# Starting every tile that matmuls read at a multiple of 128 bytes

## The chip, the cores and the metric

The kernel runs on one core of a Trainium2 chip. The metric is the device time of one execution in microseconds, and of several executions the median.

## The reference

One decoder layer, batch 1, 1024 tokens of width 1024, all in float32:

```python
h = rmsnorm(x, norm_mix)
q, kc, vc, ks, vs, kw, vw, nsa_g, rq, rk, rv, rg, gate_a, gate_b = split(h @ w_in)     # 5400 columns
nsa = NSA(rotary(q), ...)            # 8 heads of 64, 2 key groups: compressed blocks, selected blocks, window of 512
ret = retention(rotary(rq), rotary(rk), rv)   # 4 heads of 128, chunks of 128 tokens
mix = sigmoid(gate_a) * (nsa @ w_proj_a) + sigmoid(gate_b) * ((silu(rg) * ret) @ w_proj_b)
x = x + mix @ w_out
x = x + square(relu(rmsnorm(x, norm_mlp) @ w_up)) @ w_down        # hidden width 4096
y = rmsnorm(x, norm_final)
```

The top 16 of 16 key blocks are selected, so the selected branch is plain causal attention over all keys.

## The kernel before

**How a product is made.** Each float32 factor is split into a high part of a shorter type (`float32r`) and the rest: `wh` and `wl` from a raw weight tile `raw`, `bh` and `bl` for the 1024 x 1024 activations, `QQ` and `ql` for queries, `ph` and `pl` for probabilities. A product is then three matmuls: high by high, high by low, low by high. Every matmul goes through one helper, `mm` on line 153, `mm(o, w, m, start, stop)`: `w` is the stationary operand (up to 128 x 128, loaded into the array, PEld in the profile), `m` the moving one (128 x up to 512, streamed through it). In the profile's names the moving operand stands first, where the two have different names: `mm<-wh,bh` streams `wh` past `bh`, and `gps<-bh,wh` streams `bh` past `wh`.

```python
def dense_tok(o, j, W, k0=0, k1=KD, ticks=True):
    js = slice(j * P, (j + 1) * P)
    for k in range(k0, k1):
        h, l = W[k]
        mm(o, bh[:, k, js], h, k == 0, False)
        mm(o, bh[:, k, js], l, False, False)
        mm(o, bl[:, k, js], h, False, k == KD - 1)
```

**Stages, in the order of time.**

- Up to about 372 us: `dense_tok` multiplies tiles of 128 tokens with 512 columns of `w_in` (24 matmuls of 128 x 512 a call), for retention (two chunks of heads, each with a first loop over 8 token tiles for q and k, and a second loop for v and g), then for the compressed and selected keys and values, the window keys (280 columns), and the queries. Retention's own small matmuls (`pS`, `pO`, `pD`), transposes (`tp`, `pZ`) and the compression's matmuls (`pc`, 128 x 256) stand between calls or in the middle of one.
- 372 to 777 us: attention. Scores `S` stream keys (`KKs`, `KKw`) past `QQ` and `ql`; probabilities `pS`, `pW` are transposed against `ident` into `pt`, split into `ph`, `pl`, and streamed past `Vs`, `Vw`, `Vc` into `O`. Threes of gate matmuls (`gps`) are put between them by a written-out order.
- 777 to 864 us: the two projections, from `Ah`, `Al`, `Bh`, `Bl`.
- 864 to 964 us: `w_out` by `dense_tok` again, into `mmu`, with the second norm and its transposes.
- 964 to 1265 us: `w_up`, by seven products in place of eight (`mmu`), which stream `bh`, `bl` and `t2h` to `t4l`.
- 1265 us to the end: `w_down`, again seven products (`mmd`).

PE's order is the order of the code. The other engines' instructions are ordered by the code or by a scheduler when the program is built.

**Where tiles lie.** Tile pools take space in each partition from the left end upwards, or from the right end downwards (`side="right"`), and a pool that is closed gives its space to the next. Tiles start at multiples of 32 bytes. The left side starts at a multiple of 128 with `ident` (512 bytes), `small` (64) and `nhalf` (16, which take 32), 608 bytes in all, which is 96 more than a multiple of 128; the right end is itself 96 over a multiple of 128. Weights are split into slots of several pools in turn; up to 372 us

```python
wrx = es.enter_context(tc.tile_pool(name="wrx", bufs=3, reuse_waits="tile"))
use_ring(wrx, wring, wrx, wring, wrx)
```

so that of five slots three are in `wrx`, which lies behind the table `cret` (2848 bytes, 32 over a multiple of 128), and two in `wring`, which lies ahead of it. Where the operands of matmuls start, counted from the last multiple of 128 bytes, in the built program before:

| tiles | start before | start after |
|---|---|---|
| `bh`, `bl`, `KKs`, `KKw`, `Vs`, `Vw`, `Vc`, `qt`, `qkT`, `t2h` to `t4l` (right side) | 96 | 0 |
| `wh`, `wl` in `wring`, `wr4`, `wr5`, `wr7`; `Ah` to `Bl`; `h2` | 96 | 0 |
| `wh`, `wl` in `wrx` and `wr2` | 0 | 0 |
| `QQ`, `ql`, `ph`, `pl`, `pS`, `pW` (behind `cmp_m`, 480 bytes) | 64 | 0 |
| `ident`; retention's `qk`, `s`, `v`, `n`, `sd`, `z`; `xh`, `xl`, `hh`, `kd`, `cd` | 0 | 0 |
| first norm's `h` | 0 | 32 |
| `warm`, `one`, `irow` | 0 | 64 |

For shortness a matmul is called 0/96 where its moving operand starts at 0 and its stationary one at 96. Of the 5,528 `float32r` matmuls with 512 columns 4,632 are 96/96 before, 720 are 0/96 (all up to 372 us, `wh` in `wrx` past `bh`) and 176 are 96/64 (`S`). Of those with 256 columns `O` is 64/96 (592), and `pc` is 0/0 (96). The matmuls of 280 columns read the second half of a slot, which starts 96 bytes further on.

Of the kernel before, what the change touches and what calls it, by code (L numbers as in the profile page):

```python
# [9 lines left out]
F32 = mybir.dt.float32  # L10
F32R = mybir.dt.float32r
I32 = mybir.dt.int32
AF = mybir.ActivationFunctionType
# [4 lines left out]
P = 128  # L18
# [93 lines left out]
def hybrid_block(ctx: ExitStack, tc: tile.TileContext, a: dict, out: bass.AP):  # L112
    nc = tc.nc
    V, A, G, T = nc.vector, nc.scalar, nc.gpsimd, nc.tensor
    ctx.enter_context(tc.manual_schedule(engines={mybir.EngineType.PE}))

    cst = ctx.enter_context(tc.tile_pool(name="cst", bufs=1, reuse_waits="tile"))
    dram = ctx.enter_context(tc.tile_pool(name="scr", bufs=1, space=DRAM))
    bigs = ctx.enter_context(ExitStack())
    big = bigs.enter_context(tc.tile_pool(name="big", bufs=1, side="right", reuse_waits="tile"))  # L120
    wraw = ctx.enter_context(tc.tile_pool(name="wraw", bufs=3, reuse_waits="tile"))
    wring = ctx.enter_context(tc.tile_pool(name="wring", bufs=2, reuse_waits="tile"))
# [9 lines left out]
    bl = big.tile([P, KD, S], F32R, name="bl")  # L132
    ident = cst.tile([P, P], F32, name="ident")
    small = cst.tile([P, 16], F32, name="small")
    nhalf = cst.tile([P, 4], F32, name="nhalf")
    V.memset(nhalf, -0.5)
    clock = {"t": 0, "n": 0}
    due = []
# [94 lines left out]
    with ExitStack() as es:  # L233
        psA = es.enter_context(tc.tile_pool(name="psA", bufs=2, space=PSUM, reuse_waits="tile"))
        tabs = es.enter_context(tc.tile_pool(name="tabs", bufs=1, reuse_waits="tile"))
        cret = tabs.tile([P, P + 512 + 72], F32, name="cret")
        cosr = tabs.tile([P, NT, 64], F32, name="cosr")
        sinr = tabs.tile([P, NT, 64], F32, name="sinr")
        cosn = tabs.tile([P, NT, 8], F32, name="cosn")
# [5 lines left out]
        with ExitStack() as e1:  # L245
# [4 lines left out]
            nrm = nrms.enter_context(tc.tile_pool(name="nrm", bufs=2, side="right", reuse_waits="tile"))  # L250
# [136 lines left out]
            V.memset(warm, 0.0)  # L387
            one = nrm.tile([1, P], F32, name="one", bufs=1)
            V.memset(one, 1.0)
            irow = nrm.tile([1, 72], F32, name="irow", bufs=1)  # L390
            wps = psR.tile([P, 512], F32, name="pD")

            def keep_warm(n):
# [8 lines left out]
            def hi_w(i):  # L402
                wf[i] = new_slot()
                A.activation(wf[i][0], wr[i], AF.Copy)
# [16 lines left out]
            def turn(j, pool=None, *names):  # L421
                for q in range(2):
                    if pool is None:
                        tp = psA.tile([P, 4, P], F32, name="tp", tag="tp")
                    else:
                        tp = pool.tile([P, 4, P], F32, name=names[q])
                    tps[j, q] = tp
                    for k in range(4):
                        T.transpose(tp[:, k], hs[j][:, (4 * q + k) * P:(4 * q + k + 1) * P], ident)
# [31 lines left out]
            with tc.manual_schedule(engines=all_):  # L461
# [41 lines left out]
                ip = psR.tile([P, 2, P], F32, name="pZ")  # L503
# [5 lines left out]
                lo_x(0, 1)  # L509
                xs[3] = load_norm(3)  # L510
                turn(1)
                A.activation(cret[:, P + 512:], ip[:, 0, :72], AF.Copy)
                hi_w(2)
                hi_x(1)
                lo_x(1, 0)
# [42 lines left out]
                for j in range(NT):  # L558
                    ps = first[j] if j < 2 else psA.tile([P, 512], F32, name="mm", tag="mm")
                    if j > 1:  # L560
                        if j == NT - 1:
                            nrms.close()
                            tpb = e1.enter_context(tc.tile_pool(name="tmpb", bufs=3, side="right",
                                                                reuse_waits="tile"))
# [367 lines left out]
    with ExitStack() as e3:  # L932
        msk = e3.enter_context(tc.tile_pool(name="msk", bufs=1, reuse_waits="tile"))
# [2 lines left out]
        psO = e3.enter_context(tc.tile_pool(name="psO", bufs=1, space=PSUM, reuse_waits="tile"))  # L936
        at = e3.enter_context(tc.tile_pool(name="at", bufs=2, reuse_waits="tile"))
        edge_m = msk.tile([P, 640], F32, name="edge_m")
        cmp_m = msk.tile([P, 120], F32, name="cmp_m")
        nc.sync.dma_start(edge_m, a["c_edge"])  # L940
        nc.sync.dma_start(cmp_m, a["c_cmp"])

# [889 lines left out]
```

## Time and profile before

| | |
|---|---|
| median of 3 runs | 1578.4 us (1578.26, 1578.4, 1580.88) |
| span of the profiled execution, first to last instruction | 1578.3 us; no other time is given for it, and the runs' lowest is 1578.26 |
| PE busy | 1555.7 us, 99% of the span |
| DVE, ACT, POOL busy | 67%, 47%, 32% |
| granted PE clock | 0.998 |

A group's row gives line, engine, operation, output and inputs, rows and columns of the array, shape and count, then busy time and mean length of one in ns, then idle time before. Matmuls overlap: one is recorded until its results are out, while the next has long begun, so the pace of PE is read from the starts of neighbouring rows (the timeline) and not from the length of one. A row of the timeline gives start, length, engine, line, operation, tiles, array, shape and count.

### The profile page before, as it was taken

What the parts mean: (1) busy time and instruction counts of PE and PEld (TensorE: products, weight loads), DVE (VectorE), ACT (ScalarE), POOL (GpSimd) and SP (SyncE); (2) the same over time, 40 slices, a digit from 0 to 9 for tenths busy, and PEclk for the clock granted to TensorE, in tenths of its full rate; (3) what the DMA queues carried; (4) which work ended last, traced back from release to release, by engine and by line L of the source; (5) the groups of instructions that cost most, each with busy time, mean ns of one, the idle gap of its engine ahead of it and who ended that gap; (6) DMA issues with size and microseconds to landing.
All of it is one profiled execution on the core that took longest, in us unless ns stands there. A gap on an engine that the chain in (4) does not pass through costs nothing.

```text
span 1578.3 us, 22755 instructions
## 1 busy us (share of the span) xinstructions
PE 1555.7 (99%) x7905; PEld 1300.5 (82%) x7905; DVE 1053.1 (67%) x2148; ACT 736.5 (47%) x1639; POOL 508.5 (32%) x555
## 2 busy tenths in 40 slices
PE   9999999999999999999999999999999999999997
PEld 6888887987888888888888888888888888888886
DVE  6865663574777777777665278776666668786464
ACT  6653464663767766666522056222222244443352
POOL 4110010001333323333100012777777507723550
PEclk9999999999999999999999999999999999999999
DMA  6202100252111111111554351554444598674373
GB/s 209 80 18 64 58 32 26 71 184 84 34 48 35 54 48 42 53 48 61 177 165 134 128 178 54 162 179 158 155 152 147 179 357 277 188 252 127 127 256 123
DMA packets 98980, 194.35 MB, mean 123 GB/s; under 512 B 25834, under 2 KB 28146, under 8 KB 98866
## 3 DMA queue, kind: packets, MB, share of 16 engines
q1 hardware_dynamic: 98306, 191.07, 37.0%
q0 software_dynamic: 560, 1.84, 0.3%
q8 instruction: 62, 1.02, 0.3%
q14 instruction: 52, 0.43, 0.1%
HBM read 142.54 MB, written 50.33 MB: 122 GB/s over the span
## 4 chain that ended last, share of the span: by engine, by line
PE 83%; DVE 5%; POOL 4%; issue 3%; ACT 3%; DMA 2%; SPq 0%; POOLq 0%; ACTq 0%; DVEq 0%
PE mm L153 23%; PE mmu L153 20%; PE mmd L153 16%; PE gps L153 9%; PE S L153 4%; PE O L153 3%; PE pt L1058 2%; PE pt L1057 2%; ACT pW L1012 1%; DVE S L1003 1%; PE pO L153 1%; DVE pl L1060 1%; PE pc L153 1%; POOL ac L1730 1%; POOL raw L1688 1%
## 5 line engine op out<-in xcount | busy, mean ns | idle before, releaser
L1208 DVE TENSOR_TENSOR wl<-raw,wh 128x1024 fp32r<-128x1024 f32 x134 | 219.7, 1664 | 94.5 <-ACT wh L1207 94.5
L1207 ACT ACTIVATE wh<-raw 128x1024 fp32r<-128x1024 f32 x134 | 136.8, 1054 | 157.4 <-PE mmd L153 97.9
L153 PE MATMUL mm<-wh,bh 128*128 128x512 f32 (+1 forms) x448 | 175.9, 393 | 1.1 <-ACT n L742 1.0
L153 PE MATMUL mmd<-wl,wh 128*128 128x512 f32 x448 | 174.4, 389 | 0.1
L153 PE MATMUL mmd<-wh,wl 128*128 128x512 f32 x448 | 174.3, 389 | 0.0
L153 PE MATMUL mmd<-wh 128*128 128x512 f32 x448 | 174.3, 389 | 0.0
L153 PE MATMUL mm<-wl,bh 128*128 128x512 f32 (+1 forms) x448 | 169.9, 379 | 0.2 <-DVE wl L407 0.2
L153 PE MATMUL mm<-wh,bl 128*128 128x512 f32 (+1 forms) x448 | 168.8, 380 | 0.0
L187 POOL TENSOR_SCALAR msq<-ssq 128x1 f32<-128x1 f32 (+1 forms) x32 | 7.4, 230 | 389.6 <-ACT h L193 213.8
L1060 DVE TENSOR_TENSOR pl<-pt,ph 128x512 fp32r<-128x512 f32 (+1 forms) x160 | 103.7, 648 | 31.6 <-ACT ph L1059 29.3
L1022 POOL TENSOR_SCALAR pS<-pS,cf 128x1024 f32<-128x1024 f32 (+7 forms) x64 | 47.9, 748 | 219.2 <-DVE cf L1020 67.4
L1059 ACT ACTIVATE ph<-pt 128x512 fp32r<-128x512 f32 (+1 forms) x160 | 90.3, 567 | 55.3 <-PE pt L1058 52.6
L1003 DVE CUSTOM_DVE_ANT_0 S<-S,edge_m 128x512 f32<-128x512 f32 (+3 forms) x192 | 100.6, 530 | 14.8 <-PE S L153 12.9
L153 PE MATMUL gps<-bh,wh 128*128 128x512 f32 x256 | 108.1, 422 | 0.3 <-ACT gst L912 0.3
L153 PE MATMUL mmu<-bh,wh 128*128 128x512 f32 (+1 forms) x264 | 101.0, 383 | 0.0
L153 PE MATMUL mmu<-bl,wh 128*128 128x512 f32 (+1 forms) x264 | 100.9, 383 | 0.0
L153 PE MATMUL gps<-bh,wl 128*128 128x512 f32 x256 | 100.8, 394 | 0.0
L153 PE MATMUL gps<-bl,wh 128*128 128x512 f32 x256 | 100.8, 394 | 0.0
L153 PE MATMUL mmu<-bh,wl 128*128 128x512 f32 (+1 forms) x264 | 100.6, 383 | 0.0
L153 PEld LDWEIGHTS mm<-wh,bl 128*128 128x128 f32 x448 | 84.1, 188 | 18.3 <-DVE bl L448 0.7
L153 PEld LDWEIGHTS mmd<-wl,wh 128*128 128x128 f32 x448 | 84.1, 188 | 17.8 <-DVE wl L1208 0.5
L153 PEld LDWEIGHTS mmd<-wh 128*128 128x128 f32 x448 | 84.1, 188 | 17.6
(368 smaller groups left out, 4047.4 us busy)
## 6 DMA issues: line engine op xcount, KB each, us to landing
raw<-u_scr SPq DMA_DIRECT2D x56, 512.0 KB, 4.5
raw<-w_down SPq DMA_DIRECT2D x41, 512.0 KB, 5.1
raw<-w_up SPq DMA_DIRECT2D x32, 512.0 KB, 4.0
u_scr<-u SPq DMA_DIRECT2D x60, 256.0 KB, 4.2
u_scr<-s SPq DMA_DIRECT2D x45, 256.0 KB, 2.3
y<-w_down SPq DMA_DIRECT2D x16, 512.0 KB, 6.6
x<-x SPq DMA_DIRECT2D x8, 512.0 KB, 5.1
qt<-q_scr SPq DMA_DIRECT2D x32, 128.0 KB, 2.5
```

Source lines behind the costliest of these rows:

```text
L153: T.matmul(o, w, m, start=start, stop=stop)
L1003: V.tensor_tensor_reduce(sc, sc, mk, -0.125, BIGPOS, OP.add, OP.min, mx[:, b:b + 1])
L1012: A.activation(o, sc, AF.Exp, bias=mx[:, m:m + 1], scale=-1.0, accum_out=sums[:, b:b + 1])
L1022: G.tensor_scalar(v, v, cf[:, b:b + 1], 1.0, op0=OP.mult, op1=OP.mult)
L1057: T.transpose(tp[:, bi * 2], p0, ident)
L1058: T.transpose(tp[:, bi * 2 + 1], p1, ident)
L1059: A.activation(ph[:, :n], tp[:, :n], AF.Copy)
L1060: V.tensor_sub(pl[:, :n], tp[:, :n], ph[:, :n])
L1207: A.activation(h[:, :n], r, AF.Copy)
L1208: V.tensor_sub(l[:, :n], r, h[:, :n])
L1688: G.tensor_tensor(t, t, y12[g], op=OP.subtract)
L1730: G.tensor_tensor(t, t, x, op=OP.add)
```

## The change

A pad of 96 bytes is put at the right end, ahead of all tiles there; `nhalf` and `cret` are lengthened, so that what lies behind them on the left starts at a multiple of 128; `cmp_m` and `irow` are lengthened too. No instruction is added, removed or moved on any engine: the rows of all five engines are the same in the same order with the same waits. Only the addresses differ: the left side lies 32 bytes higher (64 higher behind `cmp_m`, 128 higher behind `cret`), the right side 96 bytes lower. What the operands' starts become is in the table above. Of all matmuls, 0/0 is then the rule; the exceptions are 64 transposes of `h`, some 20 small ones at the start, and 96 of the 280-column ones, whose moving half-slot starts at 96.

```diff
+    edge = ctx.enter_context(tc.tile_pool(name="edge", bufs=1, side="right", reuse_waits="tile"))
+    edge.tile([P, 24], F32, name="edge")
     big = bigs.enter_context(tc.tile_pool(name="big", bufs=1, side="right", reuse_waits="tile"))
...
-    nhalf = cst.tile([P, 4], F32, name="nhalf")
+    nhalf = cst.tile([P, 16], F32, name="nhalf")[:, :4]
...
-        cret = tabs.tile([P, P + 512 + 72], F32, name="cret")
+        cret = tabs.tile([P, 736], F32, name="cret")
...
-            irow = nrm.tile([1, 72], F32, name="irow", bufs=1)
+            irow = nrm.tile([1, 96], F32, name="irow", bufs=1)[:, :72]
...
-                A.activation(cret[:, P + 512:], ip[:, 0, :72], AF.Copy)
+                A.activation(cret[:, P + 512:P + 584], ip[:, 0, :72], AF.Copy)
...
-        cmp_m = msk.tile([P, 120], F32, name="cmp_m")
+        cmp_m = msk.tile([P, P], F32, name="cmp_m")[:, :120]
```

## The prediction

> **What bounds the kernel.** First the page: busy shares, granted clock, and the engines' shares of the chain that ended last.
>
> ```profile
> span 1578.3 us, 22755 instructions
> PE 1555.7 (99%) x7905; PEld 1300.5 (82%) x7905; DVE 1053.1 (67%) x2148; ACT 736.5 (47%) x1639; POOL 508.5 (32%) x555
> PEclk9999999999999999999999999999999999999999
> PE 83%; DVE 5%; POOL 4%; issue 3%; ACT 3%; DMA 2%; SPq 0%; POOLq 0%; ACTq 0%; DVEq 0%
> ```
>
> PE is the bound at a granted clock that never drops, so the change can pay only by the pace of matmuls or by PE's waits. The waits of PE, largest first:
>
> ```profile
> PE pt L1058 <- POOL pS L1022: 4.2, 7, 1.8
> PE S L153 <- ACT pS L1012: 2.2, 4, 1.0
> PE pD L153 <- DVE warm L387: 1.2, 1, 1.2
> ```
>
> They are few and short. What is left is the pace. The groups of matmuls, shapes apart, give lengths that differ by place although the shape is the same:
>
> ```profile
> L153 PE MATMUL mmd<-wl,wh 128*128 128x512 f32 x448 | 174.4, 389 | 0.1
> L153 PE MATMUL mm<-wl,bh 128*128 128x512 f32 x384 | 151.2, 394 | 0.2 <-DVE wl L407 0.2
> L153 PE MATMUL mm<-wh,bl 128*128 128x512 f32 x384 | 150.2, 394 | 0.0
> L153 PE MATMUL gps<-bl,wh 128*128 128x512 f32 x256 | 100.8, 394 | 0.0
> L153 PE MATMUL mmu<-bl,wh 128*128 128x512 f32 x248 | 96.5, 389 | 0.0
> ...
> L153 PE MATMUL O<-ph,Vs 128*128 128x256 f32 x144 | 38.8, 280 | 0.0
> ...
> L153 PE MATMUL S<-KKs,ql 128*128 128x512 f32 x48 | 19.0, 397 | 0.0
> ...
> L153 PE MATMUL pc<-wl,xh 128*128 128x256 f32 x32 | 9.0, 282 | 0.0
> ```
>
> The two products of the MLP (all 96/96) record 389 ns; `mm` (two thirds 0/96) and the gates 394, `S` (96/64) 397. What 389 means in pace stands in the timeline of PE in `w_down`: from the first row below to the last are 45 matmuls.
>
> ```profile
> 1299.79 0.39 PE L153 MATMUL mmd<-wl,wh 128*128 128x512 f32 x1
> ...
> 1309.99 0.39 PE L153 MATMUL mmd<-wl,wh 128*128 128x512 f32 x1
> ```
>
> 10.20 us over 45 is 226.7 ns; a recorded length is thus the pace plus 162. A length of 394 is a pace of 232, if nothing waits.
>
> The second timeline is one call of `dense_tok` at retention, inside a long run without a break. The 12 matmuls from the first row are 0/96, the 12 from the second 96/96, of which the third row is the eighth.
>
> ```profile
> 149.66 0.40 PE L153 MATMUL mm<-wh,bh 128*128 128x512 f32 x1
> ...
> 152.46 0.40 PE L153 MATMUL mm<-wh,bh 128*128 128x512 f32 x1
> ...
> 154.08 0.39 PE L153 MATMUL mm<-wl,bh 128*128 128x512 f32 x1
> ...
> 155.22 0.40 PE L153 MATMUL mm<-wh,bh 128*128 128x512 f32 x1
> ```
>
> 0/96: 2.80 us over 12, 233 ns. 96/96: 1.62 over 7, 231, and then 1.14 over 5, 228 within the rounding of the starts. So matmuls whose two operands start alike fall, after a while, into the pace of the MLP, and those that start differently don't. The same shows where `w_up` begins after transposes, 96/96 throughout:
>
> ```profile
> 965.36 0.40 PE L153 MATMUL mmu<-bl,wh 128*128 128x512 f32 x1
> ...
> 967.44 0.39 PE L153 MATMUL mmu<-bl,wh 128*128 128x512 f32 x1
> ...
> 969.93 0.39 PE L153 MATMUL mmu<-bh,wh 128*128 128x512 f32 x1
> ```
>
> Nine matmuls in 2.08 us, 231 ns, then eleven in 2.49, 226.4. I call the two the unsettled and the settled pace: a run needs about ten matmuls after a break to settle.
>
> **The change part by part.** It adds no work on any engine; the terms are what the new starts do.
>
> *Dense calls up to 372 us.* 1,152 matmuls of 512 columns (three `mm` groups of 384) pace at 232 (394 less 162); settled they would pace at 226.7, so 1152 x 5.3 = 6.1 us is all there is to win here. How much of it comes depends on the length of runs, which the chain of waits shows piece by piece:
>
> ```profile
> 34.72 0.87 PE tp L429 x8
> 35.59 5.59 PE mm L153 x24
> ...
> 55.48 2.78 PE mm L153 x12
> 58.26 0.44 PE tp L328 x4
> ...
> 135.94 29.20 PE mm L153 x126
> ...
> 331.87 0.28 PE L153 MATMUL pc<-wh,xh 128*128 128x256 f32 x1
> 331.98 0.28 PE L153 MATMUL pc<-wl,xh 128*128 128x256 f32 x1
> ...
> 332.58 0.39 PE L153 MATMUL mm<-wh,bh 128*128 128x512 f32 x1
> ```
>
> Counting runs in that way gives about 170 matmuls in runs of 6 (between the `pc` above), 400 in runs of 12 (second loops of retention), 90 in runs of 18, 310 in runs of 24 to 30, and 185 in two long ones. With ten unsettled at 231 and the rest at 226.7 the means are 231, 230.3, 229.1, 228.4 and 227; the gains on 232 are 1, 1.7, 2.9, 3.6 and 5 ns, and the sum is 0.2 + 0.7 + 0.3 + 1.1 + 0.9 = 3.2 us. Bounds: 0 and 6.1. PE waits for little there, and what it waits for starts from its own results, so I let the whole sum through.
>
> *Scores.* 176 at 397 less 162, 235 ns, now 96/64; alike they would be unsettled at best like the gates beside them, 232. Gain 176 x 3 = 0.5 us; bounds 0 and, settled, 1.5.
>
> *Gates.* 768 matmuls, 96/96 before, 0/0 after; they come in threes between attention's, too short to settle. Gain 0; at most 768 x 5.3 = 4.1 us, if the unlike neighbours are what unsettles them.
>
> *`O`.* 592 matmuls of 256 columns, 64/96, recorded at 280; the nearest rows that are 0/0, `pc`, at 282. Loss up to 2 ns x 592 = 1.2 us; I take 0.4, since most come in twos and fours after a break.
>
> *MLP, `w_out` and projections.* 96/96 becomes 0/0: alike before, alike after. No row of 512 columns in `float32r` is 0/0 before, so this term rests on 256 columns: the five spacings of `pc` above, 0/0, take 0.60 us, 120 ns. `w_up` has some 96/96:
>
> ```profile
> 960.90 0.28 PE L153 MATMUL mmu<-bh,wh 128*128 128x256 f32 x1
> ...
> 963.67 0.28 PE L153 MATMUL mmu<-bh,wl 128*128 128x256 f32 x1
> ```
>
> 23 spacings in 2.77 us, 120.4. The same pace with either start: I take no change. This is the largest lever, some 3,430 matmuls, so 1 ns there is 3.4 us.
>
> *ACT, DVE, DMA.* The weights' copies on ACT, 18 of the first row's 48 into slots at 0 (the ones in `wrx` and `wr2`), all of the second's at 96:
>
> ```profile
> L180 ACT ACTIVATE wh<-raw 128x1024 fp32r<-128x1024 f32 x48 | 50.6, 1058 | 58.4 <-PE mmu L153 37.0 <-PE mm L153 11.3 <-PE gps L153 4.1
> L1207 ACT ACTIVATE wh<-raw 128x1024 fp32r<-128x1024 f32 x134 | 136.8, 1054 | 157.4 <-PE mmd L153 97.9 <-POOL raw L1688 18.8 <-DMA raw<-u_scr 16.2
> ```
>
> No difference by start, and ACT idles for PE ahead of them; DVE's differences and the loads into `raw` lie beside PE too. I put these at nothing: the cover is PE, and without it the copies would cost what they cost now.
>
> *Sum.* 3.2 + 0.5 - 0.4 = 3.3 us off the span of 1578.3, which is 0.1 under the median: 1575.1. Three of the bounds (dense calls, gates, scores) reach further down than up, so I take 1574.8.
>
> [...]
>
> **The rivals.**
>
> *Nothing happens.* The pace of the dense calls could come from what stands beside them (retention's work on ACT and DVE) and not from their starts. For it: gates are 96/96 and pace at 232 all the same. Against it: the call at 149.66, where neighbours are the same and the pace changes with the slot. Time 1578.4, give or take 1.
>
> *Everything settles at once.* If unlike neighbours cause the unsettled stretches, dense calls, gates and scores all pace at 226.7: 6.1 + 4.1 + 1.5 - 0.4 = 11.3, 1567. Against it: the stretch at 965.36, where everything is 96/96.
>
> *A far larger gain.* 512 words from a start at 96 touch 17 stretches of 128 bytes, from 0 only 16. If the time goes by stretches, 0/0 paces at 16/17 of 226.7, 213, and 5,528 matmuls gain 13 ns, 72 us: 1506. For it: four matmuls of `warm`, 0/0 in bf16, pace at about (1.04 - 0.39)/3 = 217:
>
> ```profile
> 6.27 1.04 PE L153 MATMUL pD<-warm 128*128 128x512 bf16 x4
> ```
>
> Against it: 256 columns touch 9 stretches from 96 and 8 from 0, so `pc` at 0/0 would pace at 8/9 of 120.4, 107, and paces at 120; and 0/96 is slower than 96/96. [...]
>
> *Slower.* What makes 0/96 slow could be the moving operand's start at 0, not the difference. Then 0/0 is as slow as 0/96: 4,632 matmuls that are 96/96 go from about 228 to 233, and nothing is won back: up to 4632 x 5 = 23 us, 1601. For it: no row of 512 columns excludes it. Against it: `S` starts at 96 and is slowest, and `pc` at 0/0 is no slower than 96/96. It decides from 0.7 ns a matmul on, which already eats the 3.3.
>
> **How the numbers follow.** 0.2%, 3.2 us, is about what a measurement of this kernel can tell from no change; faster is under 1575.2, slower over 1581.6. Like operands settle (forecast): 0.60, by itself 1571.5 to 1577, with two thirds of it under 1575.2. Everything settles: 0.10. The far larger gain: 0.05. Nothing: 0.17. Slower: 0.08. Faster is 0.40 + 0.10 + 0.05 = 0.55; same 0.20 + 0.17 = 0.37; slower 0.08. The range leaves out the far gain, the slower case and a little of the lower edge: 1568 to 1579.
>
> **What would show it.** Right: `mm` groups at 390 to 392 in place of 394, the 12 matmuls after 149.66 in about 2.73 us, `mmd` and `mmu` still at 389, `S` near 394, `O` at 280 to 282. Wrong: `mmd` off 389 by more than 1 ns either way, `mm` still at 394 in the long run, or gates at 389.

## The result, and the profile after

The changed kernel takes 1588.56 us (median of 4 runs, 1586.16 to 1589.16), the kernel before 1579.41 beside it (4 runs, 1578.26 to 1580.88): ratio 1.0054, 95% interval 1.0043 to 1.0066. The change makes the kernel slower by about half a per cent; forecast was 1574.8, and the range ended at 1579.

The page of the changed kernel, the same four lines as before:

```profile
span 1584.4 us, 22755 instructions
PE 1563.1 (99%) x7905; PEld 1301.8 (82%) x7905; DVE 1050.4 (66%) x2148; ACT 736.2 (46%) x1639; POOL 509.3 (32%) x555
PEclk9999999999999999999999999999999999999999
PE 86%; DVE 4%; issue 4%; POOL 3%; ACT 3%; DMA 1%; POOLq 0%; ACTq 0%; DVEq 0%; SPq 0%
```

Same instructions, same clock; the span is 6.1 us longer and PE is busy 7.4 us more, while DVE, ACT and POOL are busy as long as before, within 3 us. PE's share of the chain goes up by 3 points. What PE waits for has hardly grown: its two largest waits in the list of waits are the rows below (4.2 and 2.2 us before), and no other grew by more than 0.2 us:

```profile
PE pt L1060 <- POOL pS L1024: 4.4, 7, 1.8
PE S L155 <- ACT pS L1014: 2.2, 4, 1.0
```

So the time is in the pace of matmuls. (The length of a row is not the pace: the 389 ns rows of `w_down` start 226.7 ns apart before. When a matmul's results are out, no row here shows.) The groups of the changed kernel, shapes apart; the numbers to read are the mean length of one in ns, behind the comma, and the idle time before, behind the second bar:

```profile
L155 PE MATMUL mmd<-wl,wh 128*128 128x512 f32 x448 | 174.4, 389 | 0.2 <-DVE wl L1210 0.2
L155 PE MATMUL mm<-wl,bh 128*128 128x512 f32 x384 | 150.8, 393 | 0.0
L155 PE MATMUL mm<-wh,bl 128*128 128x512 f32 x384 | 150.1, 394 | 0.0
L155 PE MATMUL gps<-bl,wh 128*128 128x512 f32 x256 | 100.8, 394 | 0.0
L155 PE MATMUL mmu<-bl,wh 128*128 128x512 f32 x248 | 98.1, 396 | 0.0
L155 PE MATMUL mmu<-wl,bh 128*128 128x512 f32 x128 | 50.5, 395 | 0.0
L155 PE MATMUL O<-ph,Vs 128*128 128x256 f32 x144 | 38.9, 281 | 0.0
L155 PE MATMUL S<-KKs,ql 128*128 128x512 f32 x48 | 19.0, 395 | 0.0
```

Two rows have gone the wrong way: `mmu<-bl,wh`, `w_up`, from 389 to 396, and `mmu<-wl,bh`, `w_out`, which was 390 in the kernel before:

```profile
L153 PE MATMUL mmu<-wl,bh 128*128 128x512 f32 x128 | 49.9, 390 | 0.0
```

`mmd`, `w_down`, which the change also takes from 96/96 to 0/0, still records 389. The timeline of PE gives the pace of `w_up` and `w_down`. First `w_up`, 41 spacings from the first row to the second, then `w_down`, 47:

```profile
980.92 0.39 PE L155 MATMUL mmu<-bh,wh 128*128 128x512 f32 x1
...
990.45 0.40 PE L155 MATMUL mmu<-bh,wl 128*128 128x512 f32 x1
...
1294.78 0.39 PE L155 MATMUL mmd<-wh 128*128 128x512 f32 x1
...
1305.43 0.39 PE L155 MATMUL mmd<-wh,wl 128*128 128x512 f32 x1
```

9.53 us over 41 is 232.4 ns, unsettled; 10.65 over 47 is 226.6, settled. Both are 0/0 by the table of starts. That `w_up` never settles shows over the whole stage, in the busy times by window (window, us, then PE, PEld, DVE, ACT and POOL with counts, clock, DMA share, GB/s), before and then after:

```profile
1010.00:1250.00 240.00, 240.00 (x1061) 198.72 (x1060) 168.15 (x192) 53.19 (x64) 171.42 (x104) 1.00 0.47 152
```

```profile
1000.00:1250.00 250.00, 250.00 (x1077) 202.68 (x1076) 170.50 (x198) 55.20 (x66) 175.14 (x104) 1.00 0.45 151
```

The counts hold the ones cut at the edges; taking about two off, 240/1059 is 226.6 ns a matmul before and 250/1075 is 232.6 after, at a clock of 1.00 in both.

The dense calls did what was forecast, in part. The twelve `wrx` matmuls that took 2.80 us before begin at the first row here, and the twelve of `wring` behind them at the second:

```profile
148.73 0.39 PE L155 MATMUL mm<-wh,bh 128*128 128x512 f32 x1
...
151.47 0.40 PE L155 MATMUL mm<-wh,bh 128*128 128x512 f32 x1
...
154.26 0.39 PE L155 MATMUL mm<-wh,bh 128*128 128x512 f32 x1
```

2.74 us in place of 2.80 for the first twelve; but the next twelve, which settled before (1.62 + 1.14 us to the row at 155.22), take 2.79 now: 232.5 ns. The two kinds of slot have changed places.

The length of each stage, from the starts of the first matmuls of neighbouring stages (attention from its first gate matmul, `w_down` to the start of its last matmul), in us; the experiments' columns are used below:

| stage | before | after | e1 | e2 | e3 | e4 | e5 | e6 | e8 |
|---|---|---|---|---|---|---|---|---|---|
| to attention | 371.00 | 368.54 | 369.32 | 367.61 | 367.75 | 370.82 | 370.71 | 368.31 | 368.96 |
| attention | 404.62 | 404.70 | 403.84 | 403.91 | 404.49 | 404.79 | 405.12 | 403.90 | 404.73 |
| projections | 87.04 | 87.06 | 87.04 | 87.04 | 87.04 | 87.07 | 87.06 | 87.04 | 87.07 |
| `w_out` | 93.95 | 95.39 | 93.41 | 93.73 | 93.76 | 95.53 | 94.81 | 93.93 | 95.39 |
| `w_up` | 307.06 | 314.02 | 307.06 | 307.10 | 307.06 | 314.03 | 315.29 | 307.08 | 314.02 |
| `w_down` | 304.84 | 304.96 | 304.82 | 304.85 | 304.79 | 304.92 | 304.87 | 304.83 | 304.92 |

-2.46 in the dense calls, +1.44 in `w_out`, +6.96 in `w_up` and +0.2 elsewhere make the +6.1 of the span. The medians lie 9.2 us apart and the two profiled spans only 6.1, since before's profiled span lies at the upper end of its kernel's (1576.8 to 1578.5 in the runs beside the experiments) and after's is the shortest of its own (1584.4; the others 1586.6 to 1587.1).

The 6.96 us of `w_up` are what is left of a larger loss. At about 1001 us the kernel before loses some 0.5 us to a wait of PE for `wl` from DVE (0.2 us of it are idle time in the list of waits). The profiles of e1, e2, e3 and e6 below, in which `w_up` settles, have this wait too; those of after, e4, e5 and e8, in which it doesn't, have none there. The slower pace by itself thus costs about 7.4 us, of which the missing wait gives some 0.5 back.

### The profile page after: what moved, and what is told of

Same layout as the page of the kernel before. It is cut to its first block, busy times and chain, and to the rows that moved or that the text cites. A ratio compares the mean times of both kernels' runs of the same rounds, so it can differ in the third digit from the quotient of the medians.

```text
span 1584.4 us, 22755 instructions
## 1 busy us (share of the span) xinstructions
PE 1563.1 (99%) x7905; PEld 1301.8 (82%) x7905; DVE 1050.4 (66%) x2148; ACT 736.2 (46%) x1639; POOL 509.3 (32%) x555
## 4 chain that ended last, share of the span: by engine, by line
PE 86%; DVE 4%; issue 4%; POOL 3%; ACT 3%; DMA 1%; POOLq 0%; ACTq 0%; DVEq 0%; SPq 0%
PE mmu L155 23%; PE mm L155 23%; PE mmd L155 16%; PE gps L155 9%; PE S L155 4%; PE O L155 3%; PE pt L1060 2%; PE pt L1059 2%; ACT pW L1014 1%; DVE S L1005 1%; PE pO L155 1%; DVE pl L1062 1%; PE pc L155 1%; POOL raw L1690 1%; POOL ac L1732 1%
## 5 line engine op out<-in xcount | busy, mean ns | idle before, releaser
L155 PEld LDWEIGHTS mmd<-wh,wl 128*128 128x128 f32 x448 | 84.1, 188 | 17.6
```

The costliest lines, as they stand in the source:

```text
L155: T.matmul(o, w, m, start=start, stop=stop)
```

## The experiments

What do the stages that lost have in common? In `w_out` and `w_up` one operand lies on the right side (`bh`, `bl`, `t2h` to `t4l`) and the other on the left (weights). In the projections and `w_down`, which kept their pace, both lie on the left. The change moves the right side by -96 bytes and the left by +32: 128 apart. Modulo 256, that is counted from the last multiple of 256 bytes, the starts are:

| tiles | before | after |
|---|---|---|
| right side | 224 | 128 |
| `wring`, `wr4`, `wr5`, `wr7` | 224 | 0 |
| `wrx` | 0 | 128 |

**Theory A**: a run settles at 226.7 ns where moving and stationary operand start alike modulo 256, and stays at 231 to 233 otherwise; where they start alike doesn't matter. **Theory B**: a start at a multiple of 128 is itself bad for one of the operands (close to the forecast's "slower" rival). **Theory C**: whether a stretch settles is an accident of timing at its first matmul and not tied to addresses.

One more rival needs no run: the moved tiles could bring PE's reads into conflict with the other engines or with DMA. In `w_up` of the changed kernel the spacings during which DVE, ACT and POOL all stand still average 233.7 ns (56 of them; 226.5 over 43 before), and those with no DMA packet under way 232.3, against 232.4 with one. So the slow pace is there without them.

### e1: the right side and the weights alike again, still at multiples of 128

Edit of the changed kernel; `small` and `nhalf` take the place of the pad, so that the right side and `wring`, `wr4`, `wr5`, `wr7` start at 128 modulo 256, and `wrx` at 0:

```diff
-    edge.tile([P, 24], F32, name="edge")
+    small = edge.tile([P, 16], F32, name="small")
+    nhalf = edge.tile([P, 4], F32, name="nhalf")
...
-    small = cst.tile([P, 16], F32, name="small")
-    nhalf = cst.tile([P, 16], F32, name="nhalf")[:, :4]
```

> From the changed kernel: small and nhalf move into the right-hand pad (same 96 bytes), so raw and the wring slots lie 128 bytes lower. All tiles that were at multiples of 128 still are; bh, bl and the weights of w_out and w_up are now equal modulo 256 (128/128), the wrx slots are not (0/128). Theory A (matmuls of 512 columns settle at 226.7 ns where both operands start at the same place modulo 256, else stay near 232): mmu back to 389 in the lines, mmd 389, mm near 393 to 394; 7.5 us less than the changed kernel, about the kernel before, ratio 0.998 to 1.002. Theory B (starting at a multiple of 128 is what unsettles mmu): mmu stays at 395, ratio 1.004 to 1.006. Theory C (whether a stretch settles is an accident of timing at its first matmul): mmu either way, not tied to addresses.

Measured 1577.4 us (11 runs) against 1579.52 for before (26 runs): ratio 0.9989, 0.998 to 0.9998. Groups of e1:

```profile
L154 PE MATMUL mm<-wl,bh 128*128 128x512 f32 x384 | 151.0, 393 | 0.0
L154 PE MATMUL mmu<-bl,wh 128*128 128x512 f32 x248 | 96.5, 389 | 0.0
```

`w_up` is back at 389 and 307.06 us, with both operands at multiples of 128. B is refuted for these. The dense calls keep unlike slots, as before; that they take 1.7 us less than in before's profile is more than A says. By the pace at the two differences (last section) 720 x 1 ns = 0.7 would be A's; the rest is not explained.

### e2: `wrx` alike as well

e1, and:

```diff
-        cret = tabs.tile([P, 736], F32, name="cret")
+        cret = tabs.tile([P, 768], F32, name="cret")
```

> The first experiment, with cret lengthened by 128 bytes, so that the wrx slots too are equal to bh and bl modulo 256 (128/128). Theory A: mmu 389, mm 390 to 391, 3 to 5 us under the kernel before, ratio 0.996 to 0.9985. Theory B: ratio 1.004 to 1.006, mmu 395. Theory C: no tie to addresses; mm not under 393.

Measured 1575.55 us (10 runs), ratio to before 0.9975, 0.9966 to 0.9984. This is the lowest median of the study, under the kernel before and the changed one. Groups of e2, and the timeline of its long dense run:

```profile
L154 PE MATMUL mm<-wl,bh 128*128 128x512 f32 x384 | 150.2, 391 | 0.2 <-DVE wl L408 0.2
L154 PE MATMUL mm<-wh,bl 128*128 128x512 f32 x384 | 149.4, 392 | 0.0
L154 PE MATMUL mmu<-bl,wh 128*128 128x512 f32 x248 | 96.5, 389 | 0.0
```

```profile
137.01 0.39 PE L154 MATMUL mm<-wh,bh 128*128 128x512 f32 x1
...
164.67 0.39 PE L154 MATMUL mm<-wh,bl 128*128 128x512 f32 x1
```

27.66 us over 122 spacings is 226.7: with all slots alike the whole run is settled from end to end, across the borders of slots where before and after both fell back.

### e3: everything alike, but not at multiples of 128

Edit of the kernel before; only `cret` grows, and `wrx` goes to 224, where the right side and `wring` are:

```diff
-        cret = tabs.tile([P, P + 512 + 72], F32, name="cret")
+        cret = tabs.tile([P, 768], F32, name="cret")
...
-                A.activation(cret[:, P + 512:], ip[:, 0, :72], AF.Copy)
+                A.activation(cret[:, P + 512:P + 584], ip[:, 0, :72], AF.Copy)
```

> From the kernel before: cret alone is lengthened to 768 columns, so that the wrx slots start at 224 modulo 256 like bh, bl and the wring slots; nothing starts at a multiple of 128 that did not before, and much no longer does. Theory A: mm 390 to 391, mmu and mmd 389, the same 3 to 5 us as the second experiment, ratio 0.996 to 0.9985. Theory B: nothing changes in mmu, mm gains or not, ratio 0.998 to 1.000. Theory C: ratio 1.000.

Measured 1576.61 us (11 runs), ratio 0.9983, 0.9974 to 0.9992; the dense calls take 367.75, e2's 367.61. Groups of e3:

```profile
L153 PE MATMUL mm<-wl,bh 128*128 128x512 f32 x384 | 150.5, 392 | 0.0
L153 PE MATMUL mmu<-bl,wh 128*128 128x512 f32 x248 | 96.5, 389 | 0.0
```

Multiples of 128 are not needed for the gain. One longer table has it.

### e4: only the right side, by 128 bytes

Edit of the kernel before; the right side goes to 96 modulo 256 and stays at 96 modulo 128, so the table of starts in the description above keeps every entry:

```diff
+    edge = ctx.enter_context(tc.tile_pool(name="edge", bufs=1, side="right", reuse_waits="tile"))
+    edge.tile([P, 32], F32, name="edge")
```

> From the kernel before: a pad of 128 bytes at the right end alone. No start modulo 128 changes on any tile, but bh, bl and t2 to t4 come to lie 128 away from the weights modulo 256 (96 and 224). Theory A: mmu 395 as in the changed kernel, mmd 389, mm 394 or 395, 7 to 9 us over the kernel before, ratio 1.004 to 1.007. Theory B: as before, ratio 1.000, since every start modulo 128 is the same. Theory C: ratio 1.000, or anything.

Measured 1589.65 us (5 runs), ratio 1.0064, 1.0051 to 1.0077. Groups of e4:

```profile
L155 PE MATMUL mmd<-wl,wh 128*128 128x512 f32 x448 | 174.4, 389 | 0.2 <-DVE wl L1210 0.2
L155 PE MATMUL mm<-wl,bh 128*128 128x512 f32 x384 | 151.7, 395 | 0.0
L155 PE MATMUL mmu<-bl,wh 128*128 128x512 f32 x248 | 97.7, 394 | 0.0
```

This is the run that decides. Nothing changes modulo 128, and the loss of the changed kernel is there, in the same stages (`w_out` 95.53, `w_up` 314.03). B and C fall: starts modulo 128 can't tell before from e4, and modulo 256 they can. The kernel loses 10.1 us, a little over the 7 to 9 expected; its dense calls gain nothing (370.82). The row of `w_up` is 394 here and 396 in the changed kernel, but it holds one matmul in three: all 512-column ones of the stage record 394.6 in both.

### e5: the right side by 64 bytes

As e4 with `edge.tile([P, 16], ...)`: the right side at 160, weights at 224.

> From the kernel before: a pad of 64 bytes at the right end alone, so that bh, bl and t2 to t4 lie 64 bytes (one way round, 192 the other) from the weights modulo 256, at 160 and 224. Theory A in its strict form (only a difference of 0 modulo 256 settles): w_up and w_out near 232 to 234 ns a matmul, mmu at 394 to 396, 7 to 10 us over the kernel before, ratio 1.004 to 1.007. Rival A2 (a difference that is a multiple of 64 other than 128 also settles, since 128 alone is bad): mmu at 389, ratio 0.999 to 1.001.

Measured 1589.33 us (4 runs) against 1579.11, ratio 1.0064, 1.005 to 1.0077. Groups of e5:

```profile
L155 PE MATMUL mmd<-wl,wh 128*128 128x512 f32 x448 | 174.4, 389 | 0.1
L155 PE MATMUL mmu<-bl,wh 128*128 128x512 f32 x248 | 97.7, 394 | 0.0
L155 PE MATMUL mmu<-wl,bh 128*128 128x512 f32 x128 | 50.1, 392 | 0.0
```

Starts 64 bytes apart don't settle either, so it isn't 128 bytes in particular that hurt. The last row is `w_out`, moving minus stationary +64: there the loss is a little over half (0.86 us against 1.44 and 1.58 in after and e4; mean pace 229.3); `w_up`, the other way round, -64, has all of it (233.3). Whether that is because of the operand that is ahead is not shown, since the order of the three matmuls differs between the two stages as well.

### e6: attention's operands alike

e2, and one small tile of attention padded, so that `ph` and `pl` start at 128 like `Vs`, `Vw` and `Vc`:

```diff
-                cf = at.tile([P, 3], F32, name="cf", bufs=4)
+                cf = at.tile([P, 16], F32, name="cf", bufs=4)[:, :3]
```

> From the second experiment, the one with all weights alike at 128: cf tiles are lengthened so that ph and pl start at 128 modulo 256 like Vs, Vw, Vc; of attention, all operands but ident and the transposes' are then alike. Theory A carried on to threes and to 256 columns: gates settle more often, attention 1 to 3 us shorter, ratio to the kernel before 0.9955 to 0.9975. Rival (with 256 columns it doesn't matter, and threes of gates are too short): attention within 0.5 us of the second experiment, O within 2 ns of 280, ratio 0.997 to 0.998.

Measured 1576.33 us (11 runs), ratio to before 0.998, 0.9971 to 0.9989; attention takes 403.90 us, in e2 403.91. Groups of e6, and of e2 below:

```profile
L154 PE MATMUL gps<-bl,wh 128*128 128x512 f32 x256 | 100.5, 392 | 0.0
L154 PE MATMUL O<-ph,Vs 128*128 128x256 f32 x144 | 38.7, 280 | 0.0
```

```profile
L154 PE MATMUL O<-ph,Vs 128*128 128x256 f32 x144 | 38.6, 279 | 0.0
```

Carrying A on to attention was wrong. `O`, with 256 columns, shows no effect of how its operands start: they are 96 apart modulo 256 before, alike in after and e6 and 128 apart in e2, and neighbouring `O` start 117 to 118 ns apart in all four. The gates were alike in e2 already; at 392 to 393, with nearly all their neighbours alike in e6, they don't settle in their runs of three.

The dense calls of e6 have e2's starts and take 368.31 us against 367.61. One wait of PE for `wl`, 0.8 us in place of 0.2, is most of it. So this stage is known from one profile to some 0.7 us only.

### e7: the high and low halves of a slot unlike

e1, with 128 bytes between `wh` and `wl` of a slot, so that even in `w_down` some operands are unlike:

```diff
         h = pool.tile([P, 1024], F32R, name="wh", tag="wh")
+        pool.tile([P, 32], F32, name="gap", tag="gap", bufs=1)
         l = pool.tile([P, 1024], F32R, name="wl", tag="wl")
```

> From the first experiment: in every pool of split weights a gap of 128 bytes is put between the wh and the wl tiles, so that high and low part of a weight are unlike modulo 256. In w_down every group of 24 matmuls is then one of two kinds. Kind 1: high parts of both operands alike; own operands are alike in one matmul of three, but what streams and the weights that are loaded meanwhile for the next matmul are alike in all three. Kind 2: high parts unlike; own operands alike in two of three, stream and next weights unlike in all three. Theory A1 (what counts is the running stream against the weights that are being loaded for the next matmul): kind 1 settles at 226.7 ns, kind 2 stays at 232. Theory A2 (what counts are a matmul's own two operands): neither settles wholly, and kind 2, with fewer unlike ones, is the faster. Span not compared.

One run: 1593.08 us, span 1591.2. A1 has it that a stream must be like the weights loaded while it runs, those of the next matmul (in `w_down` of the kernel before, the load for the matmul of 1300.24 us is recorded at 1300.02 for 0.19 us, beside the matmul that starts at 1300.01); A2 that it must be like its own. Timeline of `w_down` in e7; from the first row 24 matmuls of which two in three are like their own weights and none but the last is like the next (kind 2 of the expectation), from the second 24 of which one in three is like its own and all but the last are like the next (kind 1):

```profile
1290.71 0.39 PE L154 MATMUL mmd<-wh 128*128 128x512 f32 x1
...
1296.22 0.40 PE L154 MATMUL mmd<-wh 128*128 128x512 f32 x1
...
1301.76 0.39 PE L154 MATMUL mmd<-wh 128*128 128x512 f32 x1
```

5.51 us, 229.6 ns, and 5.54, 230.8. Over all of `w_down` the 40 groups of the first sort average 229.4 (228.9 to 229.6) and the 13 of the second 231.1. By A1 the second would be settled and the first not at all, so A1 falls. In the first, once it has run a while, the unlike one of three takes 232 and the two alike 226 and 228. That speaks for a matmul's own two operands. Not cleanly: in the second even the matmul that is like its own takes 230 on average, so neighbours matter as well.

### e8: the changed kernel again, unchanged

> The changed kernel once more, for a second profile: its first profiled execution was the shortest of four (span 1584.4, the others 1586.6 to 1587.1). Theory A: w_up and w_out unsettled as before (mmu 394 to 396), w_down and projections settled; the further 2 us lie in a part that sometimes settles and sometimes doesn't, the dense calls up to 372 us with their three unlike and two alike slots in five. Rival: they are waits, on DMA or another engine, not pace. Ratio 1.004 to 1.007.

1586.99 us (4 runs) against 1579.17, ratio 1.0051, 1.0034 to 1.0068. `w_out` takes 95.39 and `w_up` 314.02, as in the first profile to 0.01 us, and the group of `w_up` is the same:

```profile
L155 PE MATMUL mmu<-bl,wh 128*128 128x512 f32 x248 | 98.1, 396 | 0.0
```

The loss belongs to the kernel. Its size was 9.2 us of the medians at first and is 7.8 here; the two profiled spans, 1584.4 and 1584.8, less before's usual 1577.4 are 7.0 and 7.4. The expectation sought the further 2 us of the first measurement's other runs in the dense calls. They take 0.4 us more here than in the first profile (368.96), and two of PE's waits there are 0.7 us longer together; but this profile too is of a short execution, so where the one or two us lie stays open.

## Why the prediction was wrong, point by point

- **The failed step** is "*MLP, `w_out` and projections.* 96/96 becomes 0/0: alike before, alike after", priced at no change and named as the largest lever. The table of starts was taken modulo 128; the measured pace goes with the starts modulo 256 (226.7 ns alike, 232.4 at 128 apart). There `w_out` and `w_up` go from 224/224 to 0/128 and 128/0, unlike, and the price is 1.44 + 6.96 = 8.4 us. e4 shows that it is this and not the starts modulo 128. The support of the term, 256 columns pacing at 120 with either start, carried nothing. Both of its rows were alike modulo 256, so they couldn't show what unlike starts do; and the 256-column ones here don't react to them: those of `w_up` come to lie 128 apart in the changed kernel and still start 120 ns apart (119.8 before), as `O` doesn't react in e6. The warning was in the sentence itself: no row of 512 columns was 0/0.
- **Dense calls**: the mechanism was right and so was the sum for runs that are alike throughout, 3.2 us forecast, 3.4 in e2, 3.25 in e3 and 2.7 in e6. That it fits so well is partly luck: this stage is known to some 0.7 us only, and e1 gained 1.7 with its slots still unlike. In the changed kernel 2.5 came (2.0 in e8): the `wrx` slots gained it, as the twelve at 148.73 show (2.73 forecast, 2.74 measured), and the `wring` slots turned unlike, so runs never stay settled for long.
- **Gates**, forecast 0: they go from alike to unlike. Where gate follows gate without a break their pace goes from 232.0 to 233.1, and all spacings behind gates add up to 0.4 us more. **Scores**, forecast -0.5: -0.3, but not by becoming alike: modulo 256 their operands were 32 apart and are now 128 apart. **`O`**, forecast +0.4: the mean length goes from 280 to 281, but the spacings add up to -0.3. Together attention stays within 0.1 us.
- **ACT, DVE, DMA** at nothing: right in the main; no wait of PE grew by more than 0.2 us, and the one in `w_up` went away.
- **The rivals.** "Slower" had the sign and named its price per matmul nearly rightly (5 ns; 232.4 less 226.7 is 5.7), for the wrong reason: with the moving operand at 0 `w_down` still runs at 226.6. "Everything settles at once" is excluded by the gates in e2 (393 though alike), the "far larger gain" by `mmd` at 389. "Nothing happens" is excluded by e2 and e3.

## What to carry to other kernels

When a pace depends on two addresses, tabulate their difference and try several moduli: the alignment that was tidy for each operand alone was the wrong one for the pair here. Long runs of 512-column `float32r` matmuls ran at 226.7 ns where moving and stationary operand start at the same place modulo 256 bytes, and at 229.3 to 233.9 at the six other differences seen; whether that place is a multiple of 128 made no difference (e2 and e3: dense calls 367.61 and 367.75 us, `mmu` 389 in both). A pad at one end of the partition was enough to lose 10.1 us (e4), one longer table to win 2.9 (e3). And the largest lever of a sum needs a row of its own shape: a row of another shape that shows no effect is no evidence for this one.

## What the runs showed of the hardware

Mean spacing of 512-column `float32r` matmuls that stand later than the twelfth of a run, by moving minus stationary start modulo 256 bytes, over before, after and e1 to e6, all at a granted clock of 0.998 to 0.999:

| difference | 0 | 32 | 64 | 96 | 128 | 160 | 192 |
|---|---|---|---|---|---|---|---|
| ns | 226.7 | 233.4 | 229.3 | 233.5 | 232.4 | 233.9 | 233.3 |

The columns 32 (before), 96 (e5) and 160 (e4) rest on 170 spacings each, of `wrx` slots; 64 and 192 come from e5 alone; so only 0 and 128 are seen in more than one kernel. The pace of alike operands is the same at 0 (after's `w_down`), 128 (e2) and 224 (before). In e2 pairs whose starts differ by an odd multiple of 256 bytes settle like those that differ by an even one (226.7 both), as `w_up` and `w_down` do in before (226.7 both), so the period is 256 or a part of it, and e4, e5 and the column 32 exclude 128, 64 and 32. In the kernel before, settling took about nine matmuls after a break (231 ns from 965.36 us, then 226.4) and about seven after a change of slot (231 from 152.46, then 228); unlike ones at 128 repeat a cycle of seven spacings (231, 232, 228, 230, 233, 241, 232 ns, mean 232.4) through all of `w_up` in after, e4 and e8. Matmuls of 256 columns start some 117 to 120 ns apart, alike or not (`O` 117 to 118 in before, after, e2 and e6; those of `w_up` 119.8 before and 120 after). What makes unlike starts slower no run here shows; e7 says only that a matmul's own pair seems to matter and its neighbours' to some extent (229.4 ns for groups with two in three like their own, 231.1 with one in three).
